# Value tiles of a first normalization: products taken by part, stage order and one load's queue changed

## Chip, core and metric

The kernel runs on one core of a Trainium2 chip, one launch of one program. The metric is the time of an execution on the device in microseconds (us), the median of several runs. Five engines work beside each other, each through its own instructions in order: TensorE (PE in the profile: matrix products and transposes, into PSUM banks), VectorE (DVE), ScalarE (ACT), GpSimd (POOL) and SyncE (SP, which here issues all DMAs).

## What is computed

The reference is one block of a streaming encoder in float32, over 1024 tokens and 16 meta tokens of 1024 channels:

```
u = rmsnorm(h, norm_mix)                    # h: 16 meta tokens, then 1024 tokens
z = u @ w_in                                # a, q, k, v, r, lr, ga, gb
y_a = pooling mixer of a;  y_b = chunked gated linear attention of q, k, v, lr, gated by r
h = h + (sigmoid(ga) * y_a + sigmoid(gb) * y_b) @ w_out
h = h + relu(rmsnorm(h, norm_ffn) @ w_ff1)^2 @ w_ff2
out = rmsnorm(h, norm_final)[16:]
```

The change lies in the first line and in the first columns of the second: the normalization of the tokens, and the products that make half of v (256 columns) and lr (16 columns).

## The kernel before

Each float32 operand is held as two parts, a high part (rounded by a ScalarE copy) and a low part (the rest, by a VectorE subtraction). A product takes three matmuls: high x high, high x low, low x high (`mm3`, L241 to L248). In the tables below `th`, `tl` are the high and low part of the normalized, transposed tokens, `vw` those of the value weights, `w1h`, `w1l` those of the gate weights.

The tokens come in eight tiles of 128 (t = 0 to 7; the 16 meta tokens are t = 8). One tile takes these steps:

- `squared(t)`: ScalarE squares the tile (1024 columns) and sums by row (L578); the next step of the same generator, `first_rms`, takes logarithm and exponential on ScalarE (L580, L581) and then a few operations on columns of one element (L582 to L590), on VectorE for t = 0 and 1, on GpSimd above that. The result is the row's scale `rs[t]`; `rest(t)` fetches it.
- `normed(t)`: VectorE multiplies the tile by `rs[t]` into one of three buffers `us` (L631), SP reloads its slot with tile t+4, TensorE transposes the tile in eight pieces into two banks (`turned`, L550).
- `taken(b, t)`: for each of the two banks VectorE multiplies by the norm's weights, a column per channel (`gcol`; L557, to `ut`), and ScalarE copies the high part (L566). It hands back the function that makes the low part on VectorE (L567).
- `v_tile(0, t)`: TensorE multiplies the tile by the value weights, 24 matmuls of 272 columns. It hands back two functions that copy the bank out on ScalarE (L497, L501).

ScalarE, VectorE and GpSimd run in the written order in this stage (`tc.manual_schedule`). In pass t of the loop the order is: the matmuls of tile t; `normed(t+2)`; the copying out of tile t-1; `rest(t+3)` (logarithm, exponential, small operations); `taken` of tile t+1; `squared(t+4)`; the low parts of tile t+1. Passes 5, 6 and 7 also split the first four pieces of gate weights (`q.prime`; L264 on ScalarE, L265 on VectorE). Before the loop stand tiles 0 and 1, the two dummy runs of transposes of the identity (`warm(12)`, `warm(10)`, L639), the transposing of the norm's weights into `gcol` (L656, L657), and the splitting of the value weights (`load_vw`: `hi` L455, `lo` L458, `lr` L462 and L463 for the low-rank columns).

SP issues, in this order at the start: tile 0, the identity, the norm's weights, tile 1, two blocks of value weights, the low-rank columns (`lrraw`, 1024 pieces of 64 bytes), tiles 2 and 3.

Behind the loop `differences` prepares the operands of a Strassen-like scheme for the gates: the tokens' quarters in `ut` are subtracted in place (`differ`, L726), and split into P5, P6, P7 and P4 (`halved`: L720 on ScalarE, L721 on VectorE). Between these steps `next(run)` issues one product each (`Quarters.run`): the split of the weights three products ahead, 12 matmuls, and evictions (L361).

Of the kernel before, what the change touches and what calls it, by code (L numbers as in the profile page):

```python
# [12 lines left out]
ALU = mybir.AluOpType  # L13
AX = mybir.AxisListType

P = 128
D = 1024
SEQ = 1024
META = 16
# [11 lines left out]
NPAIR = DFF // P // 2  # L31
MP = 264
PACE, LEVEL = 1.1, 1.6
WARM = (12, 10)


class Stack:
# [68 lines left out]
def kernel(  # L106
# [84 lines left out]
    def f32(ap):  # L191
        return ap.bitcast(F32)
# [256 lines left out]
    def load_vw(i, raws=None, parts=False):  # L449
        vw, raws = S["vw"][i], raws or fetch_vw(i)  # L450
        c = [slice(j * P, (j + 1) * P) for j in range(2)]
        eng = pool if i else dve

        def hi(j):
            act.activation(vw[:, 0, :, c[j]], raws[j], ACT.Copy)  # L455

        def lo(j):
            eng.tensor_tensor(vw[:, 1, :, c[j]], raws[j], f32(vw[:, 0, :, c[j]]), ALU.subtract)  # L458

        def lr():  # L460
            r = S["lrraw"]
            act.activation(vw[:, 0, :, 256:], r, ACT.Copy)  # L462
            dve.tensor_tensor(vw[:, 1, :, 256:], r, f32(vw[:, 0, :, 256:]), ALU.subtract)  # L463

        if parts:
            return hi, lo, lr
        for j in range(2):
            hi(j)
            lo(j)

    vm = gB[32 : 32 + META, : 2 * 256]

    def v_tile(i, t, later=False):

        vw, w = S["vw"][i], 256 + 16 * (i == 0)
        if t == 8:
            half, at, n = 0, 0, META
        else:
            half, n = t // 4, P
            at = OFF[half] + (t % 4) * P  # L480
        b = bank("mm")[:n, :w]
        th, tl, hi, lo = TH[half][:, :, at : at + n], TL[half][:, :, at : at + n], vw[:, 0], vw[:, 1]
        if i == t == 0:

            for k in range(KT):
                pe.matmul(b, th[:, k], hi[:, k], start=k == 0, stop=False)
                pe.matmul(b, tl[:, k], hi[:, k], start=False, stop=False)
            for k in range(KT):
                pe.matmul(b, th[:, k], lo[:, k], start=False, stop=k == KT - 1)
        else:  # L490
            mm3(b, KT, lambda k: (th[:, k], tl[:, k]), lambda k: (hi[:, k], lo[:, k]))

        def leave():
            if t == 8:
                act.activation(vm[:, i * 256 : i * 256 + 256], b[:, :256], ACT.Copy)
            else:
                act.activation(S["v"][i][:, t], b[:, :256], ACT.Copy)  # L497

        def leave_lr():
            if i == 0:  # L500
                act.activation(S["lrtok"][:n, t], b[:, 256:], ACT.Copy)  # L501

        if later:
            return leave, leave_lr
        leave()
        leave_lr()
# [64 lines left out]
    def first_rms(xt, u, eng):  # L571

        rows = xt.shape[0]
        rs_n[0] += 1
        k = rs_n[0] % 2
        ss = ln_stat[rs_n[0] % 4][:rows]
        y, v, t = (stat[2 * k][:rows, 4 * i : 4 * i + 1] for i in range(3))
        act.activation(u, xt, ACT.Square, accum_out=ss)  # L578
        yield ss
        act.activation(y, ss, ACT.Ln, scale=1.0 / D, bias=eps_t[:rows])  # L580
        act.activation(y, y, ACT.Exp, scale=-0.5)  # L581
        eng.tensor_scalar(v, ss, -0.5 / D, -0.5 * EPS, ALU.mult, ALU.add)  # L582
        if eng is dve:
            dve.scalar_tensor_tensor(t, v, y, y, ALU.mult, ALU.mult)
            dve.scalar_tensor_tensor(ss, t, 1.5, y, ALU.add, ALU.mult)
        else:
            eng.tensor_tensor(t, v, y, ALU.mult)
            eng.tensor_tensor(t, t, y, ALU.mult)
            eng.tensor_scalar(t, t, 1.5, None, ALU.add)
            eng.tensor_tensor(ss, t, y, ALU.mult)  # L590
        yield ss

    def start():
# [25 lines left out]
        nc.sync.dma_start(g8, norm_mix.rearrange("(k p) -> k p", p=P))  # L619
        load(1)  # L620
        raws = fetch_vw(0)
        nc.sync.dma_start(S["lrraw"], w_in[:, C_LR : C_LR + 16].rearrange("(k p) c -> p k c", p=P))
        load(2)
        load(3)
        m = lambda half, j: tuple(a[half][:, 4 * j : 4 * j + 4, OFF[half] : OFF[half] + HALF] for a in (TH, TL))
# [2 lines left out]
        def normed(t):  # L628

            x_, u = of(t)  # L630
            dve.tensor_scalar(u, x_, rs[t], None, ALU.mult)  # L631
            if t < 4:
                load(t + 4)
            return turned(u)

        def warm(n):

            for _ in range(n):
                pe.transpose(idle[:, :P], ident, ident)  # L639
# [4 lines left out]
        with tc.manual_schedule(engines={mybir.EngineType.Activation, mybir.EngineType.DVE, mybir.EngineType.Pool}):  # L644
            rs, rms, b, leave = {}, {}, {}, None

            def squared(t):
                rms[t] = first_rms(xm if t == 8 else xs[:, t % 4], us[: META if t == 8 else P, t % 3], pool if t > 1 else dve)
                next(rms[t])

            def rest(t):
                rs[t] = next(rms[t])

            warm(WARM[0])
            bg = bank("ms")
            pe.transpose(bg[:, :KT], g8, ident[:KT, :KT])  # L656
            dve.tensor_copy(gcol, bg[:, :KT])  # L657
            squared(0)
            rest(0)
            b[0] = normed(0)  # L660
            squared(1)
            part = taken(b[0], 0)
            lows = [next(part)]
            rest(1)
            lows.append(next(part))
            b[1] = normed(1)
            warm(WARM[1])
            for fn in lows:
                fn()
            hi, lo, lr = load_vw(0, raws, True)  # L670
            for j in range(2):
                hi(j)
                lo(j)
            lr()
            squared(2)
            rest(2)
            squared(3)
            for t in range(8):
                left_now, leave = leave or (nothing,) * 2, v_tile(0, t, True)
                if t < 6:  # L680
                    b[t + 2] = normed(t + 2)
                if t < 2:
                    q.load(t, 0)
                elif t == 2:
                    nc.sync.dma_start(xm, meta)
                    q.load(0, 1)
                    q.load(1, 1)
                    nc.sync.dma_start(mf, masks)
                elif t == 7:
                    dve.tensor_scalar(xm, xm, rs[8], None, ALU.mult)  # L690
                for fn in left_now:
                    fn()
                if t < 6:
                    rest(t + 3)
                lows = list(taken(b[t + 1], t + 1)) if t < 7 else []
                if t < 5:
                    squared(t + 4)
                for fn in lows:
                    fn()
                for n in {5: (0,), 6: (1, 2), 7: (3,)}.get(t, ()):  # L700
                    q.prime(n == 0)
            differ((0, 0), (1, 0), (0, 0))
            bm = bank("ms")[:, : 8 * META].rearrange("p (a b) -> p a b", a=8)
            for i in range(KT):
                pe.transpose(bm[:, i], xm[:, i * P : (i + 1) * P], ident[:META, :META])
            um = us[:, 0, : 8 * META].rearrange("p (a b) -> p a b", a=8)
            for j in range(2):
                weighted(um[:, 4 * j : 4 * j + 4], bm[:, 4 * j : 4 * j + 4], j)
            th, tl = (a[0][:, :, :META] for a in (TH, TL))
            act.activation(th, um, ACT.Copy)  # L710
            dve.tensor_tensor(tl, um, f32(th), ALU.subtract)
            pool.tensor_copy(mask, mf)
            differences(run, leave)
# [9 lines left out]
    def differ(to, a, b):  # L723
        for k in range(0, 4, 2):
            to_, a_, b_ = (S["ut"][j][:, k : k + 2] for j in (to, a, b))
            dve.tensor_tensor(to_, a_, b_, ALU.subtract)  # L726

    def differences(run, values):


        b11, b21, b12, b22 = (0, 0), (0, 1), (1, 0), (1, 1)
        left.pop_to(S["left_x"])
        halved("P5", b11)
        for fn in values:
            fn()
        next(run)
        leave = v_tile(0, 8, True)
        differ(b11, b22, b11)
        next(run)
        for fn in leave:  # L740
            fn()
        halved("P6", b11)
        next(run)
        differ(b12, b22, b12)
        lr_turn()
        next(run)
        right.pop_to(S["right_ut"][4])
        halved("P7", b12)
        next(run)
        differ(b21, b21, b11)  # L750
        right.pop_to(S["right_ut"][2])
        halved("P4", b21)
        next(run)
        right.pop_to(S["right_ut"][0])
# [380 lines left out]
    def part(i):  # L1135
        return slice(i * CH, (i + 1) * CH)
# [562 lines left out]
```

## Time and profile before

| | |
|---|---|
| median of 3 runs | 1243.65 us (1243.61 to 1248.66) |
| profiled execution | 1241.63 us |
| its span | 1239.6 us, 18265 instructions |
| busy in the span | PE 97%, DVE 69%, ACT 50%, POOL 5% |
| mean granted TensorE clock | 0.996 |

The profile's page has the shares of the span; the views of the trace answer for a stretch of it. A timeline row gives start and duration in us, engine, line, operation, what it writes and reads, how many are merged, and in brackets the engine's idle time before it with what ended it. A row of waits gives the total, the number and the longest. A row of stages (from:to) gives its length, each engine's busy time with the number of instructions, the granted TensorE clock, the DMA engines' busy share and GB/s.

### The profile page before, as it was taken

How to read it: one execution, taken by the hardware profiler on the slowest of the kernel's cores; microseconds unless marked ns; L12 is line 12 of the kernel's file. 1: busy time of each engine (PE TensorE's matmuls, PEld its weight loads, DVE VectorE, ACT ScalarE, POOL GpSimd, SP SyncE). 2: the span in 40 equal slices, each digit the busy share in tenths (PEclk: the TensorE clock that was granted, in tenths of full speed). 3: DMA queues.
4: the chain of work that ended last, by engine and by line, in shares of the span. 5: the costliest groups of instructions: out<-in, count | busy, mean ns of one | idle time of the engine just before them, and what ended most of it. 6: DMA issues, size and time to landing. Idle time of an engine off the chain costs nothing.

```text
span 1239.6 us, 18265 instructions
## 1 busy us (share of the span) xinstructions
PE 1206.1 (97%) x6816; PEld 1003.1 (81%) x6816; DVE 850.9 (69%) x1388; ACT 618.8 (50%) x1099; POOL 66.6 (5%) x74
## 2 busy tenths in 40 slices
PE   7999999999999999899999999999999999999997
PEld 6878888988887778688878888888887788888886
DVE  6896676654556676634896676776774877887686
ACT  6667567322446663412654454555553444444554
POOL 2100000001101015400000000000000000000000
PEclk9999999999999999899999999999999999999999
DMA  8033326146102247831244444444569863333432
GB/s 250 2 110 104 110 86 193 53 155 219 36 19 78 69 133 234 282 109 51 98 125 159 156 153 143 162 156 134 176 216 374 289 235 102 94 99 98 162 98 89
DMA packets 142680, 173.84 MB, mean 140 GB/s; under 512 B 10968, under 2 KB 82416, under 8 KB 142592
## 3 DMA queue, kind: packets, MB, share of 16 engines
q1 hardware_dynamic: 142592, 172.68, 43.3%
q8 instruction: 53, 0.87, 0.3%
q14 instruction: 35, 0.29, 0.1%
HBM read 119.17 MB, written 53.48 MB: 139 GB/s over the span
## 4 chain that ended last, share of the span: by engine, by line
PE 85%; DVE 8%; ACT 3%; DMA 2%; issue 2%; SPq 0%; DVEq 0%; ACTq 0%
PE b_mm L246 10%; PE b_mm L247 10%; PE b_mm L248 10%; PE b_ms L247 9%; PE b_ms L246 9%; PE b_ms L248 9%; PE b_x L248 8%; PE b_x L246 8%; PE b_x L247 8%; PE b_sc L1147 1%; PE b_ms L550 1%; PE b_mx L246 1%; PE b_m L1249 1%; PE b_mx L247 1%; PE b_mx L248 1%
## 5 line engine op out<-in xcount | busy, mean ns | idle before, releaser
L246 PE MATMUL b_mm<-th,w1h 128*128 128x512 f32 (+1 forms) x312 | 117.6, 377 | 1.9 <-DVE c L761 1.1
L247 PE MATMUL b_mm<-tl,w1h 128*128 128x512 f32 (+1 forms) x312 | 116.0, 372 | 0.6 <-DVE tl L1407 0.6
L248 PE MATMUL b_mm<-th,w1l 128*128 128x512 f32 (+1 forms) x312 | 115.8, 371 | 0.0
L246 PE MATMUL b_x<-th,w1h 128*128 128x512 f32 (+1 forms) x240 | 90.8, 378 | 0.0
L247 PE MATMUL b_x<-tl,w1h 128*128 128x512 f32 (+1 forms) x240 | 90.6, 378 | 0.0
L248 PE MATMUL b_x<-th,w1l 128*128 128x512 f32 (+1 forms) x240 | 90.3, 376 | 0.0
L264 ACT ACTIVATE w1h<-raw 128x512 fp32r<-128x512 f32 x96 | 59.6, 621 | 36.8 <-PE b_x L247 14.1
L265 DVE TENSOR_TENSOR w1l<-raw,w1h 128x512 fp32r<-128x512 f32 x96 | 65.6, 684 | 12.9 <-ACT w1h L264 12.9
L246 PEld LDWEIGHTS b_mm<-th,w1h 128*128 128x128 f32 x312 | 58.6, 188 | 13.7 <-issue 1.8
L264 ACT ACTIVATE w1h<-fs 128x512 fp32r<-128x512 f32 x72 | 45.4, 631 | 45.8 <-PE b_ms L247 31.5
L247 PEld LDWEIGHTS b_mm<-tl,w1h 128*128 128x128 f32 x312 | 58.6, 188 | 10.6 <-DVE tl L1407 0.9
L248 PEld LDWEIGHTS b_mm<-th,w1l 128*128 128x128 f32 x312 | 58.6, 188 | 10.3
L264 ACT ACTIVATE w1h<-bt 128x512 fp32r<-128x512 f32 x44 | 27.8, 632 | 67.7 <-issue 59.6
L265 DVE TENSOR_TENSOR w1l<-fs,w1h 128x512 fp32r<-128x512 f32 x72 | 49.3, 685 | 14.7 <-ACT w1h L264 14.6
L1556 DVE TENSOR_TENSOR bt<-w,w 128x512 f32<-128x512 f32 x80 | 54.6, 683 | 1.0 <-DMA w<-in_w_ff_dram 1.0
L248 PEld LDWEIGHTS b_x<-th,w1l 128*128 128x128 f32 x240 | 45.1, 188 | 8.4
L246 PEld LDWEIGHTS b_x<-th,w1h 128*128 128x128 f32 x240 | 45.0, 188 | 8.5
L247 PEld LDWEIGHTS b_x<-tl,w1h 128*128 128x128 f32 x240 | 45.1, 188 | 8.3
L264 ACT ACTIVATE fxh<-bt 128x512 fp32r<-128x512 f32 x36 | 22.8, 632 | 55.4 <-issue 48.1
L246 PE MATMUL b_ms<-wo,w1h 128*128 128x512 f32 x128 | 49.8, 389 | 0.0
L247 PE MATMUL b_ms<-wo,w1h 128*128 128x512 f32 x128 | 49.8, 389 | 0.0
L248 PE MATMUL b_ms<-wo,w1l 128*128 128x512 f32 x128 | 49.8, 389 | 0.0
(446 smaller groups left out, 3365.2 us busy)
## 6 DMA issues: line engine op xcount, KB each, us to landing
hf_dram<-h SPq DMA_DIRECT2D x112, 256.0 KB, 2.1
raw<-hf_dram SPq DMA_DIRECT2D x112, 256.0 KB, 2.7
w<-in_w_ff_dram SPq DMA_DIRECT2D x64, 256.0 KB, 4.9
raw<-in_w_in_dram SPq DMA_DIRECT2D x24, 512.0 KB, 4.9
raw<-in_w_ff_dram SPq DMA_DIRECT2D x16, 512.0 KB, 4.1
rawx<-in_w_ff_dram SPq DMA_DIRECT2D x16, 512.0 KB, 4.1
xs<-in_x_dram SPq DMA_DIRECT2D x8, 512.0 KB, 4.7
rawx<-in_w_in_dram SPq DMA_DIRECT2D x8, 512.0 KB, 4.7
```

The source lines that it names most:

```text
L246: pe.matmul(ps, ah, bh, start=first and i == 0, stop=False, skip_group_check=more)
L247: pe.matmul(ps, ah, bl, start=False, stop=False, skip_group_check=more)
L248: pe.matmul(ps, al, bh, start=False, stop=last and i == n - 1, skip_group_check=more)
L264: act.activation(hi, a, ACT.Copy)
L265: dve.tensor_tensor(lo, a, f32(hi), ALU.subtract)
L550: pe.transpose(b[j][:, i], u[:, (4 * j + i) * P : (4 * j + i + 1) * P], ident)
L1147: pe.matmul(b[to, e, j], kk[r, s], qq[r, s], start=True, stop=True, tile_position=(e * CH, u * CH))
L1249: pe.matmul(o[part(u), e, j], scc[part(u), e, j], v[part(u), j, e], start=j == 0, stop=False, tile_position=(u * CH, u * CH), skip_group_c ...
L1556: dve.tensor_tensor(bt, w, S["w2"][q[3:]][:, i], ALU.add if q[2] == "+" else ALU.subtract)
```

## The change

- `first_rms` yields once more, after logarithm and exponential, so that `squared`, `root` and `rest` are three steps. Tile 2's small operations go to VectorE too.
- Before the loop: dummy runs of 4, 8 and 12; the copy to `gcol` behind `normed(0)`; tile 1's root ahead of tile 0's high parts; the weights' high parts ahead, and their low parts behind the weighting of tile 1. The matmuls of tiles 0 and 1 are issued by part (high x high, low x high, high x low, eight each) among these steps, with `normed(2)` between them. Squares, roots and small operations of tiles 2 and 3 are there as well.
- The loop starts at t = 1. In pass t the order is now: the matmuls of tile t (t > 1); `normed(t+2)`; the copying out of tile t-1; `taken` of tile t+1; square, root and small operations of tile t+3; the low parts of tile t+1.
- `lrraw` is loaded by a DMA on GpSimd's queue.
- In `differences` the split of P6 comes one product earlier.

```diff
--- before.py
+++ after.py
@@ -31,7 +31,7 @@
 NPAIR = DFF // P // 2
 MP = 264
 PACE, LEVEL = 1.1, 1.6
-WARM = (12, 10)
+WARM = (4, 8, 12)
 
 
 class Stack:
@@ -460,7 +460,7 @@
         def lr():
             r = S["lrraw"]
             act.activation(vw[:, 0, :, 256:], r, ACT.Copy)
-            dve.tensor_tensor(vw[:, 1, :, 256:], r, f32(vw[:, 0, :, 256:]), ALU.subtract)
+            return lambda: dve.tensor_tensor(vw[:, 1, :, 256:], r, f32(vw[:, 0, :, 256:]), ALU.subtract)
 
         if parts:
             return hi, lo, lr
@@ -470,7 +470,7 @@
 
     vm = gB[32 : 32 + META, : 2 * 256]
 
-    def v_tile(i, t, later=False):
+    def v_tile(i, t, later=False, by_part=False):
 
         vw, w = S["vw"][i], 256 + 16 * (i == 0)
         if t == 8:
@@ -480,14 +480,16 @@
             at = OFF[half] + (t % 4) * P
         b = bank("mm")[:n, :w]
         th, tl, hi, lo = TH[half][:, :, at : at + n], TL[half][:, :, at : at + n], vw[:, 0], vw[:, 1]
-        if i == t == 0:
-
+        parts = {"hh": (th, hi), "lh": (tl, hi), "hl": (th, lo)}
+        left_of = {"n": 3}
+
+        def part(name):
+            left_of["n"] -= 1
+            l, r = parts[name]
             for k in range(KT):
-                pe.matmul(b, th[:, k], hi[:, k], start=k == 0, stop=False)
-                pe.matmul(b, tl[:, k], hi[:, k], start=False, stop=False)
-            for k in range(KT):
-                pe.matmul(b, th[:, k], lo[:, k], start=False, stop=k == KT - 1)
-        else:
+                pe.matmul(b, l[:, k], r[:, k], start=name == "hh" and k == 0, stop=left_of["n"] == 0 and k == KT - 1)
+
+        if not by_part:
             mm3(b, KT, lambda k: (th[:, k], tl[:, k]), lambda k: (hi[:, k], lo[:, k]))
 
         def leave():
@@ -500,6 +502,8 @@
             if i == 0:
                 act.activation(S["lrtok"][:n, t], b[:, 256:], ACT.Copy)
 
+        if by_part:
+            return part, (leave, leave_lr)
         if later:
             return leave, leave_lr
         leave()
@@ -579,6 +583,7 @@
         yield ss
         act.activation(y, ss, ACT.Ln, scale=1.0 / D, bias=eps_t[:rows])
         act.activation(y, y, ACT.Exp, scale=-0.5)
+        yield ss
         eng.tensor_scalar(v, ss, -0.5 / D, -0.5 * EPS, ALU.mult, ALU.add)
         if eng is dve:
             dve.scalar_tensor_tensor(t, v, y, y, ALU.mult, ALU.mult)
@@ -619,7 +624,7 @@
         nc.sync.dma_start(g8, norm_mix.rearrange("(k p) -> k p", p=P))
         load(1)
         raws = fetch_vw(0)
-        nc.sync.dma_start(S["lrraw"], w_in[:, C_LR : C_LR + 16].rearrange("(k p) c -> p k c", p=P))
+        pool.dma_start(S["lrraw"], w_in[:, C_LR : C_LR + 16].rearrange("(k p) c -> p k c", p=P))
         load(2)
         load(3)
         m = lambda half, j: tuple(a[half][:, 4 * j : 4 * j + 4, OFF[half] : OFF[half] + HALF] for a in (TH, TL))
@@ -645,7 +650,10 @@
             rs, rms, b, leave = {}, {}, {}, None
 
             def squared(t):
-                rms[t] = first_rms(xm if t == 8 else xs[:, t % 4], us[: META if t == 8 else P, t % 3], pool if t > 1 else dve)
+                rms[t] = first_rms(xm if t == 8 else xs[:, t % 4], us[: META if t == 8 else P, t % 3], pool if t > 2 else dve)
+                next(rms[t])
+
+            def root(t):
                 next(rms[t])
 
             def rest(t):
@@ -654,29 +662,51 @@
             warm(WARM[0])
             bg = bank("ms")
             pe.transpose(bg[:, :KT], g8, ident[:KT, :KT])
-            dve.tensor_copy(gcol, bg[:, :KT])
+            warm(WARM[1])
             squared(0)
+            root(0)
             rest(0)
             b[0] = normed(0)
+            dve.tensor_copy(gcol, bg[:, :KT])
             squared(1)
-            part = taken(b[0], 0)
-            lows = [next(part)]
+            root(1)
+            lows = [list(taken(b[0], 0))]
             rest(1)
-            lows.append(next(part))
+            warm(WARM[2])
             b[1] = normed(1)
-            warm(WARM[1])
-            for fn in lows:
+            hi, lo, lr = load_vw(0, raws, True)
+            hi(0)
+            hi(1)
+            lr_lo = lr()
+            v0, leave0 = v_tile(0, 0, by_part=True)
+            v1, leave = v_tile(0, 1, by_part=True)
+            v0("hh")
+            for fn in lows[0]:
                 fn()
-            hi, lo, lr = load_vw(0, raws, True)
+            v0("lh")
+            lows.append(list(taken(b[1], 1)))
+            v1("hh")
             for j in range(2):
-                hi(j)
                 lo(j)
-            lr()
+            lr_lo()
+            v0("hl")
             squared(2)
+            root(2)
             rest(2)
+            b[2] = normed(2)
+            v1("hl")
+            for fn in lows[1]:
+                fn()
+            v1("lh")
             squared(3)
-            for t in range(8):
-                left_now, leave = leave or (nothing,) * 2, v_tile(0, t, True)
+            root(3)
+            rest(3)
+            q.load(0, 0)
+            for t in range(1, 8):
+                if t > 1:
+                    left_now, leave = leave, v_tile(0, t, True)
+                else:
+                    left_now = leave0
                 if t < 6:
                     b[t + 2] = normed(t + 2)
                 if t < 2:
@@ -690,11 +720,11 @@
                     dve.tensor_scalar(xm, xm, rs[8], None, ALU.mult)
                 for fn in left_now:
                     fn()
+                lows = list(taken(b[t + 1], t + 1)) if t < 7 else []
                 if t < 6:
+                    squared(t + 3)
+                    root(t + 3)
                     rest(t + 3)
-                lows = list(taken(b[t + 1], t + 1)) if t < 7 else []
-                if t < 5:
-                    squared(t + 4)
                 for fn in lows:
                     fn()
                 for n in {5: (0,), 6: (1, 2), 7: (3,)}.get(t, ()):
@@ -736,10 +766,10 @@
         next(run)
         leave = v_tile(0, 8, True)
         differ(b11, b22, b11)
+        halved("P6", b11)
         next(run)
         for fn in leave:
             fn()
-        halved("P6", b11)
         next(run)
         differ(b12, b22, b12)
         lr_turn()
```

## The prediction

> **What bounds the kernel now.** I read the head of the profile's page, then TensorE's waits, then its busy time by stage.
>
> ```profile
> span 1239.6 us, 18265 instructions
> PE 1206.1 (97%) x6816; PEld 1003.1 (81%) x6816; DVE 850.9 (69%) x1388; ACT 618.8 (50%) x1099; POOL 66.6 (5%) x74
> ```
>
> TensorE is busy in all but 33.5 us of the span, and the change keeps every real product. It can only take from these 33.5 us, or add to them. Two views say where they lie near the change: waits (us in total, times, longest) and stages (from:to, length, busy time of each engine).
>
> ```profile
> PE b_ms L248 <- DVE w1l L265: 1.8, 1, 1.8
> ...
> PE b_mm L246 <- DVE c L761: 1.1, 1, 1.1
> ```
> ```profile
> 4.60:17.50 12.90, 8.49 (x38) 7.67 (x39) 7.31 (x16) 7.76 (x17) 0.33 (x1) 1.00 0.93 281
> 17.50:47.20 29.70, 29.70 (x244) 29.55 (x243) 26.58 (x42) 22.33 (x57) 10.75 (x37) 1.00 0.44 114
> 47.20:76.50 29.30, 27.58 (x139) 21.69 (x139) 25.65 (x33) 19.39 (x34) 0.00 (x0) 1.00 0.04 15
> ```
>
> The real products begin at about 17.5. From there to 47.2 (the eight value tiles) TensorE never stops; then it stops twice, 1.8 us at P4's product and 1.1 us behind a bank, both times for VectorE. So there are three places to look at: the start, the loop over tiles (full, so it can only lose), and the two stops.
>
> **1. The start: the normalization of tile 3 comes 2.8 us earlier.** Timeline rows: start, duration, engine, line.
>
> ```profile
> 6.00 0.20 ACT L581 ACTIVATE small<-small 128x1 f32<-128x1 f32 x1
> 7.70 0.17 DVE L657 COPY small<-b_ms 128x8 f32<-128x8 f32 x1 [6.83 <-PE b_ms L656]
> 7.79 0.14 DVE L582 TENSOR_SCALAR small<-small 128x1 f32<-128x1 f32 x1
> 8.05 0.22 DVE L584 SCALAR_TENSOR_TENSOR small<-small 128x1 f32<-128x1 f32 x1
> 8.50 0.75 DVE L631 TENSOR_SCALAR us<-xs,small 128x1024 f32<-128x1024 f32 x1
> 9.31 1.97 PE L550 MATMUL b_ms<-ident,us 128*128 128x128 f32 x8 [1.64 <-DVE us L631]
> 13.85 1.99 ACT L455 ACTIVATE vw<-raw 128x1024 fp32r<-128x1024 f32 x2
> 15.06 2.35 DVE L458 TENSOR_TENSOR vw<-raw,vw 128x1024 fp32r<-128x1024 f32 x2
> 15.95 1.04 ACT L578 ACTIVATE us<-xs 128x1024 f32<-128x1024 f32 x1
> 17.55 1.04 ACT L578 ACTIVATE us<-xs 128x1024 f32<-128x1024 f32 x1
> 18.85 0.75 DVE L631 TENSOR_SCALAR us<-xs,small 128x1024 f32<-128x1024 f32 x1 [1.23 <-POOL small L590]
> ```
>
> The root of tile 0 is ready at 6.2, but VectorE first waits for the copy of the weights' column (7.70), behind 12 dummy transposes. The change moves that copy behind the normalization. From L584 to L631 is 0.45, so normalization 0 starts at about 6.7, 1.8 earlier; its transposes, 0.81 later, at 7.5, end at 9.5. The second half is weighted by 10.2, three small operations (7.79 to 8.50: 0.71) give normalization 1 at 10.9, and its transposes stand by 12.7. Meanwhile ScalarE makes the weights' high parts, 1.99, from 10.8 to 12.8, and the low-rank columns. VectorE takes the low parts of tile 0 (1.28) to 12.8 and then weights tile 1. By the loop's rows below (26.03 to 27.88) the next square starts 1.85 later, at 14.65; the square after it 1.60 later (15.95 to 17.55), at 16.25; and from a square to its normalization by way of GpSimd it is 2.90 (15.95 to 18.85). By ScalarE, then, normalization 3 could start at 19.15. VectorE has ahead of it: tile 1 weighted (to 14.05), the weights' low parts and the low-rank ones (2.35 and 0.25, to 16.65), tile 2's small operations, which leave GpSimd (0.71, to 17.4), normalization 2 (0.66, to 18.05), tile 1's low parts (1.28). That is **19.3**, which I take; before it was 22.11.
>
> The 24 dummies (22 before) lie where TensorE is idle (8.49 of 12.90 us busy, and 22 dummies are in that): nothing. Were the 12 behind tile 0 still at 0.21 each (1.97 for eight, against 1.04 below), tile 1's transposes would be some 0.4 late, under VectorE's 1.28: nothing either.
>
> Tiles 0 and 1 by part: the same 48 products in another order, at a time when normalization 3, not TensorE, sets what comes next: nothing. One gate weight's load is issued before the loop, not in it; its split is at 38.71 (below): nothing.
>
> The low-rank load: its row in the DMA view (KB, us to landing), and its issue.
>
> ```profile
> lrraw<-in_w_in_dram SPq DMA_DIRECT2D x1, 64.0 KB, 7.2
> ```
> ```profile
> 3.54 3.02 SPq L622 DMA_DIRECT2D lrraw<-in_w_in_dram  x1
> ```
>
> SP is spared 3.02 us of issue, and tiles 2 and 3 load that much earlier; but the square of tile 2 (15.95) shows no wait for its load, so that is worth nothing. On GpSimd's queue I take the same 7.2 us from about 1.1, behind its first memsets: 8.3, against a need at 12.8. Bounds: nothing, or, beyond 4.5 us of delay, one for one, because ScalarE works in order and the first product, tile 1 and the next squares stand behind that copy.
>
> [...]
>
> **2. The loop: it loses its look-ahead.** Before, pass t squares tile t+4 and takes the root of tile t+3, squared one pass ago. After, pass t does square, roots and GpSimd's operations of tile t+3, all behind ScalarE's copies of tile t+1; and the first thing VectorE does in pass t+1 is normalization t+3. That is an added wait. Behind it on VectorE stand the weighting and the low parts of tile t+2, for which TensorE's tile t+2 waits.
>
> ```profile
> 20.70 1.04 PE L550 MATMUL b_ms<-ident,us 128*128 128x128 f32 x8
> 22.11 0.75 DVE L631 TENSOR_SCALAR us<-xs,small 128x1024 f32<-128x1024 f32 x1
> 24.56 1.04 PE L550 MATMUL b_ms<-ident,us 128*128 128x128 f32 x8
> 25.37 0.75 DVE L631 TENSOR_SCALAR us<-xs,small 128x1024 f32<-128x1024 f32 x1
> 26.03 1.28 DVE L557 TENSOR_TENSOR ut<-b_ms,small 128x512 f32<-128x512 f32 x2
> 27.88 1.04 ACT L578 ACTIVATE us<-xs 128x1024 f32<-128x1024 f32 x1
> 35.55 0.75 DVE L631 TENSOR_SCALAR us<-xs,small 128x1024 f32<-128x1024 f32 x1
> 38.71 0.62 ACT L264 ACTIVATE w1h<-rawx 128x512 fp32r<-128x512 f32 x1
> 39.78 0.68 DVE L265 TENSOR_TENSOR w1l<-rawx,w1h 128x512 fp32r<-128x512 f32 x1
> 40.11 1.03 PE L550 MATMUL b_ms<-ident,us 128*128 128x128 f32 x8
> 40.75 1.29 DVE L557 TENSOR_TENSOR ut<-b_ms,small 128x512 f32<-128x512 f32 x2 [0.29 <-PE b_ms L550]
> ```
>
> A pass now takes TensorE (40.11 - 24.56) / 4 = 3.89. The new circle: normalization to the square behind the copies, 25.37 to 27.88 = 2.51; square to the normalization that it feeds, 2.90; together **5.41**. No step of it overlaps another, since every engine works in order. So normalization 7 starts at 19.3 + 4 x 5.41 = 40.95 (before 35.55), the square of pass 5 at 43.45. Then in order: the split of the first gate weight on ScalarE, 1.60 later at 45.05, 0.62; its low part on VectorE, 0.6 to the next; the weighting of tile 7 at about 46.35 instead of 40.75. VectorE is **5.6** us late. TensorE's tile 7 waits for its low parts (46.35 + 1.28 + 0.1 + 0.64 = 48.35), and 21 products remain. A pass of 3.89, less 1.0 of transposes, by 24 gives 0.12 for one: the last starts at 50.9, against 40.11 + 1.0 + 48 x 0.12 = 46.9 before, **4.0** late.
>
> **3. P6's split: VectorE gets 2.5 us back.**
>
> ```profile
> 52.63 2.35 DVE L726 TENSOR_TENSOR ut<-ut,ut 128x1024 f32<-128x1024 f32 x2
> 55.51 0.68 DVE L265 TENSOR_TENSOR w1l<-fs,w1h 128x512 fp32r<-128x512 f32 x1
> 58.76 2.36 DVE L721 TENSOR_TENSOR P6l<-ut,P6h 128x1024 fp32r<-128x1024 f32 x2 [2.57 <-ACT P6h L720]
> 63.07 0.40 PE L246 MATMUL b_mm<-P5h,w1h 128*128 128x512 f32 x1
> 76.57 0.51 PE L248 MATMUL b_ms<-P4h,w1l 128*128 128x512 f32 x1 [1.78 <-DVE w1l L265]
> 80.26 0.47 PE L246 MATMUL b_mm<-th,w1h 128*128 128x512 f32 x1 [1.10 <-DVE c L761]
> ```
>
> P6h stood on ScalarE behind two evictions that waited for TensorE; now it follows the difference (52.63), half by half, and VectorE's wait of 2.57 shrinks to about 0.1. The split of P5's weights falls behind it by 2 us; its product is at 63.07, its split ended at 56.2 (55.51 + 0.68): covered. VectorE feeds both stops of TensorE, so what counts at 76.57 is VectorE's lateness: 5.6 - 2.5 = 3.1. TensorE by itself would be 4.0 - 1.8 = 2.2 late there. The later decides: **+3.1**. The stop behind the bank moves along, and what follows keeps its relative order.
>
> **The sum.** Start -2.8 and loop +8.4 on VectorE make +5.6; P6 -2.5; so +3.1 us. The profiled execution, 1241.63 (span 1239.6 and 2.03 around it), would be 1244.7. The median of the runs shown is 1243.65, 2.0 above it; on it I forecast **1246.8**, slower by 0.25%. I call 0.5% (6.2 us) about what a measurement of this kernel can tell from no change, so this counts as the same.
>
> **Rivals.**
> - *TensorE stays the bound of the loop.* That needs ScalarE's squares to run ahead of the copies in front of them; all of the trace's rows are in program order, which speaks against it. Then tile 2's normalization at 17.4, transposes at 18.2 to 19.25, 16 products of 0.12, and tile 3's transposes at 21.2 instead of 24.56: -3.3, and both stops gone (-2.9): 1237.4. 12%.
> - *P6's move gives nothing*, because P6h now waits for TensorE in another way or VectorE's idle time returns before P4: +5.6, 1249.3. 12%.
> - *The clock falls in the loop* (ends slower). A circle of 5.41 leaves TensorE 1.4 us idle per pass. The trace shows one drop:
>
> ```profile
> 515.00:527.00 12.00, 6.76 (x19) 4.49 (x19) 9.23 (x9) 5.33 (x7) 3.80 (x3) 0.72 0.92 305
> ```
> ```profile
> 521.25 0.79 PE L246 MATMUL b_mm<-wo,th 128*128 128x512 f32 x1 [2.83 <-ACT wo L1345]
> ```
>
> There TensorE was 56% busy, its gaps up to 2.83, and the granted clock averaged 0.72: 12 x 0.28 = 3.4 us lost. In the loop it would be 3.9 / 5.41 = 72% busy with gaps of about 1 us. If that sufficed it would cost 3.4 on top: 1250.2. It decides as soon as the busy share falls near 56%. 10%.
>
> [...]
> - *The low-rank load lands late* (ends slower): beyond 12.8 one for one; 4 us more give 1250.8. 8%.
>
> **How the numbers follow.** My forecast has 58%, by itself 1244 to 1249 (the profiled execution and the median differ by 2.0, and the circle by 0.2 a pass). With the second rival, part of the third and some of the fourth the range 1242 to 1251 holds 8 in 10; below it lies the first rival, above it the rest of the last two. Faster than 1237.4: half the first rival, 6%. Slower than 1249.9: most of the third and of the fourth, and the ends of the second and of the forecast, 17%. The rest, 77%, is the same.
>
> **What the changed profile would show.** Right: normalizations (L631) near 6.7, 10.9 and 19.3, then one every 5.4 us, each ended by GpSimd; TensorE waiting about 1.5 us a pass from tile 3 on; no wait at P6l; P4's wait under 1 us, near 79.7. Wrong: tile transposes every 3.9 us; ScalarE waiting for lrraw; products of 0.25 us in the loop; a wait of more than 2 us still at P4.

## The result, and the profile after

The changed kernel takes 1248.44 us (median of 22 runs, 1245.84 to 1251.81); the kernel before, run beside it, 1245.62 (22 runs). The ratio is **1.0021, 95% interval 1.0012 to 1.0031**: 2.6 us slower (1.5 to 3.9). The forecast was +3.1 us. In what follows line numbers are those of the changed kernel, 4 or 5 higher at the start and 30 higher behind the loop.

The head of the page of the changed kernel; its execution took 1250.37 us.

```profile
span 1248.6 us, 18265 instructions
PE 1211.1 (97%) x6818; PEld 1004.1 (80%) x6818; DVE 852.0 (68%) x1391; ACT 618.5 (50%) x1099; POOL 63.9 (5%) x70
```

This span is 9.0 us longer than the one before, over three times what the medians differ by. So the two spans aren't compared; I follow one instruction of both traces instead, the product behind the bank at P4, which was at 80.26. TensorE's timeline after:

```profile
67.98 0.40 PE L246 MATMUL b_mm<-P5h,w1h 128*128 128x512 f32 x1
...
80.18 0.50 PE L248 MATMUL b_ms<-P4h,w1l 128*128 128x512 f32 x1 [0.70 <-DVE w1l L265]
...
83.88 0.47 PE L246 MATMUL b_mm<-th,w1h 128*128 128x512 f32 x1 [1.13 <-DVE c L791]
```

P5's first product is 4.91 us later than before (63.07), P4's third 3.61 (76.57), the one behind the bank 3.62. From there the shift hardly moves: +3.54 at about 500 us. That is what the change costs, and the medians agree with it. The stages, as in the prediction:

```profile
4.60:17.50 12.90, 11.05 (x73) 9.78 (x73) 9.83 (x23) 10.63 (x23) 0.36 (x1) 1.00 1.06 337
17.50:47.20 29.70, 25.80 (x185) 22.70 (x184) 18.55 (x30) 16.60 (x44) 6.79 (x31) 1.00 0.38 94
47.20:76.50 29.30, 28.13 (x151) 22.61 (x152) 28.03 (x37) 19.44 (x36) 0.47 (x2) 1.00 0.00 1
```

At the start TensorE does more (73 matmuls for 38), in the loop's stage less: 185 for 244, with all of 29.70 us busy before. VectorE's timeline shows why:

```profile
6.99 0.75 DVE L636 TENSOR_SCALAR us<-xs,small 128x1024 f32<-128x1024 f32 x1
...
10.58 0.75 DVE L636 TENSOR_SCALAR us<-xs,small 128x1024 f32<-128x1024 f32 x1
...
19.44 0.75 DVE L636 TENSOR_SCALAR us<-xs,small 128x1024 f32<-128x1024 f32 x1 [0.67 <-POOL small L595]
...
24.86 0.75 DVE L636 TENSOR_SCALAR us<-xs,small 128x1024 f32<-128x1024 f32 x1 [2.07 <-POOL small L595]
...
41.32 0.75 DVE L636 TENSOR_SCALAR us<-xs,small 128x1024 f32<-128x1024 f32 x1 [2.14 <-POOL small L595]
...
46.76 1.28 DVE L561 TENSOR_TENSOR ut<-b_ms,small 128x512 f32<-128x512 f32 x2
...
58.63 2.35 DVE L756 TENSOR_TENSOR ut<-ut,ut 128x1024 f32<-128x1024 f32 x2
61.04 2.36 DVE L751 TENSOR_TENSOR P6l<-ut,P6h 128x1024 fp32r<-128x1024 f32 x2
...
64.64 0.69 DVE L317 TENSOR_TENSOR fs<-fs,rawx 128x512 f32<-128x512 f32 x1
```

Each normalization of the loop now begins after an idle stretch of about 2.1 us that GpSimd ends, 5.42 to 5.50 us after the last one. The chain that ends last, asked for the stretch to 50 us, walks once round the circle per pass:

```profile
24.86 0.75 DVE us L636
25.61 0.61 DVE ut L561
26.25 1.23 ACT th L570 x2
27.47 1.05 ACT us L582 x2
30.34 0.75 DVE us L636
```

Normalize, weight, copy the high parts, square the next tile, its scale (the stretch from 28.5 to 30.34, too small pieces for this list), normalize again: no TensorE in it. TensorE's own idle time shows far less of it:

```profile
PE b_ms L554 <- DVE us L636: 3.4, 6, 1.0
PE b_mm L248 <- DVE tl L571: 1.3, 6, 0.2
```

In the loop that is 0.52 to 0.58 and 0.21 us a pass (the 1.0 belongs to tile 1, ahead of the loop), though a pass takes 1.6 us more than before. The other half hides in the modelled ends: a product lasts 0.29 us in the records and the next starts 0.125 later, so of the 0.50 us between the starts at 27.16 and 27.66 only 0.21 counts as idle. The starts of two equal instructions tell the pass's length; the idle column doesn't.

### The profile page after: what moved, and what is told of

Read it like the earlier page. It is cut to its first block, busy times and chain, and to the rows that moved or that the text cites. A ratio compares the mean times of both kernels' runs of the same rounds, so it can differ in the third digit from the quotient of the medians.

```text
span 1248.6 us, 18265 instructions
## 1 busy us (share of the span) xinstructions
PE 1211.1 (97%) x6818; PEld 1004.1 (80%) x6818; DVE 852.0 (68%) x1391; ACT 618.5 (50%) x1099; POOL 63.9 (5%) x70
## 4 chain that ended last, share of the span: by engine, by line
PE 83%; DVE 9%; ACT 4%; DMA 2%; issue 1%; POOL 0%; SPq 0%; ACTq 0%; DVEq 0%; POOLq 0%
PE b_mm L246 10%; PE b_mm L247 9%; PE b_mm L248 9%; PE b_ms L246 9%; PE b_ms L247 9%; PE b_ms L248 9%; PE b_x L248 8%; PE b_x L246 8%; PE b_x L247 8%; PE b_sc L1177 1%; PE b_mx L246 1%; PE b_mx L247 1%; PE b_mx L248 1%; DMA raw<-hf_dram 1%; DVE ut L756 1%
```

## Experiments

The theory: **the loop's lost look-ahead makes the circle of 5.4 us, and P6's earlier split gives part of it back at P4.** The rivals: the cost is at the start (the load on GpSimd's queue, the dummies); or P6's move does nothing; or the price lies in the clock. Each run is read twice: by its ratio to the kernel before, and by the shift of the product behind the bank (before 80.26).

**a_ahead: the change with the look-ahead given back.**

```diff
             rest(3)
+            squared(4)
             q.load(0, 0)
...
-                lows = list(taken(b[t + 1], t + 1)) if t < 7 else []
                 if t < 6:
-                    squared(t + 3)
                     root(t + 3)
                     rest(t + 3)
+                lows = list(taken(b[t + 1], t + 1)) if t < 7 else []
+                if t < 5:
+                    squared(t + 4)
```

> The changed kernel with the look-ahead given back: tile 4 squared before the loop, then in pass t the roots and small operations of tile t+3 ahead of the copies of tile t+1, and the square of tile t+4 behind them. Theory (the circle of the loop costs what is lost): normalizations 3.9 us apart instead of 5.4, TensorE without waits in the loop, P4's third product some 6 us ahead of the kernel before (near 70.5 instead of 76.57), time 5 to 6 us below before, ratio about 0.9955. Rival (the products by part or the load on GpSimd's queue cost it): that product stays behind the kernel before, near 79 to 80, ratio about 1.002.

Measured: 1238.71 us (5 runs) against 1243.68 (15), ratio **0.9957 (0.9944 to 0.997)**. Its profile, in turn VectorE's normalizations, TensorE's timeline, and one stretch of the loop:

```profile
22.94 0.75 DVE L636 TENSOR_SCALAR us<-xs,small 128x1024 f32<-128x1024 f32 x1
26.20 0.75 DVE L636 TENSOR_SCALAR us<-xs,small 128x1024 f32<-128x1024 f32 x1
```
```profile
59.96 0.40 PE L246 MATMUL b_mm<-P5h,w1h 128*128 128x512 f32 x1
...
71.30 0.39 PE L248 MATMUL b_ms<-P4h,w1l 128*128 128x512 f32 x1
...
74.77 0.47 PE L246 MATMUL b_mm<-th,w1h 128*128 128x512 f32 x1 [1.04 <-DVE c L793]
```
```profile
20.00:43.00 23.00, 22.79 (x186) 22.50 (x185) 21.82 (x35) 17.54 (x44) 7.92 (x27) 1.00 0.39 96
```

The waits for GpSimd are gone, normalizations follow every 3.26 us (3.9 was expected; VectorE runs ahead of TensorE), and TensorE is busy in 22.79 of 23.00 us. P5's first product is 3.11 us earlier than before (the start's gain, kept through the loop), and P4's stop has vanished too: -5.49 behind the bank. A few moved lines turn 3.6 us lost into 5.5 gained. The loop's order is the cost, and the rest of the change is worth having.

**c_loop: the loop's new order alone, in the kernel before.**

```diff
             squared(3)
+            rest(3)
...
-                if t < 6:
-                    rest(t + 3)
                 lows = list(taken(b[t + 1], t + 1)) if t < 7 else []
-                if t < 5:
-                    squared(t + 4)
+                if 0 < t < 6:
+                    squared(t + 3)
+                    rest(t + 3)
```

> The kernel before with only the order of the loop changed: square, roots and small operations of tile t+3 all behind the copies of tile t+1 in pass t, none ahead; tile 3's are done before the loop. Theory: normalizations 5.4 us apart from tile 3 on, normalization 7 near 43.7 instead of 35.55, P4's third product 8.3 us late (near 84.9), ratio about 1.0067. Rival (the loop hides most of the circle): under 3 us late, ratio under 1.0025.

Measured: 1250.63 us (4 runs) against 1243.68, ratio **1.0054 (1.0041 to 1.0068)**. Normalizations, then P4's third product:

```profile
22.18 0.75 DVE L631 TENSOR_SCALAR us<-xs,small 128x1024 f32<-128x1024 f32 x1
27.66 0.76 DVE L631 TENSOR_SCALAR us<-xs,small 128x1024 f32<-128x1024 f32 x1 [2.15 <-POOL small L590]
```
```profile
84.27 0.51 PE L248 MATMUL b_ms<-P4h,w1l 128*128 128x512 f32 x1 [1.80 <-DVE w1l L265]
```

The same circle, 5.48 us, from the old start: P4 is 7.70 late, the product behind the bank 7.71 (87.97), and +8.1 remain at about 500 us; somewhat less than the 8.3 expected, since VectorE's wait at P6l is 1.48 here instead of 2.57. (A clock drop at 85 us, with products 0.43 us apart for 0.23 and a granted clock of 0.93 over 76.5 to 100, stands here in place of the bank's stop.) With the old start and the old place of P6's split little else pays it back.

**d_no_p6: the change with P6's split at its old place.**

```diff
-        halved("P6", b11)
         next(run)
         for fn in leave:
             fn()
+        halved("P6", b11)
```

> The changed kernel with the split of P6 put back to its old place. Theory: VectorE has no wait of 2.57 us to lose, P4's third product comes 2.5 us later than in the changed kernel (near 82.7), ratio to the kernel before 1.0045. Rival (the move gives nothing): as the changed kernel, 80.2, ratio 1.002.

Measured: 1250.43 us (4 runs) against 1243.68, ratio **1.0054 (1.0039 to 1.007)**. VectorE at P6, TensorE at P4:

```profile
63.92 2.36 DVE L751 TENSOR_TENSOR P6l<-ut,P6h 128x1024 fp32r<-128x1024 f32 x2 [1.48 <-ACT P6h L750]
```
```profile
81.73 0.51 PE L248 MATMUL b_ms<-P4h,w1l 128*128 128x512 f32 x1 [1.80 <-DVE w1l L265]
```

P4 comes at 81.73, 5.16 after the kernel before; the prediction's sum without P6 was 5.6. The changed kernel has it at 80.18, 1.55 earlier; at about 500 us the difference is 1.82 (shift +5.36 against +3.54, with a clock drop at 82 to 85 us in this run, products 0.43 us apart for 0.23). But 0.25 of it is there at normalization 3 (19.69 for 19.44), far ahead of the edit, and stays up to P5's first product (68.23 for 67.98): the move is worth 1.3 at P4. The ratios, 1.0054 and 1.0021, are 4 us apart, but their intervals allow from 1 to 7. VectorE's wait for P6h is 1.48 here, not the 2.57 of the kernel before: VectorE arrives 6 us later, TensorE only 5, and with it the evictions that held P6h up. The wait had already shrunk.

**b_p6: P6's split moved, in the kernel before.** The same edit as in d_no_p6, the other way round.

> The kernel before with only the split of P6 moved forward. Theory: VectorE's wait of 2.57 us at P6l goes, P4's third product comes 1.8 us earlier without a wait and the stop behind the bank shrinks as well, together 2.5 to 2.9 us, ratio about 0.998. Rival (the move gives nothing): VectorE waits elsewhere before P4, ratio 1.000.

Measured: 1241.86 us (11 runs) against 1243.68, ratio **0.9982 (0.9973 to 0.9991)**.

```profile
74.61 0.39 PE L248 MATMUL b_ms<-P4h,w1l 128*128 128x512 f32 x1
...
78.06 0.47 PE L246 MATMUL b_mm<-th,w1h 128*128 128x512 f32 x1 [1.03 <-DVE c L761]
```

P4's stop of 1.78 has gone, and the whole is 2.20 earlier, somewhat less than the 2.5 to 2.9 expected: as the stop is gone, TensorE itself sets the limit. The rival that P6's move gives nothing falls.

**e_lr_sp and f_ahead_lr_sp: the low-rank load back on SP's queue**, in the change and in a_ahead.

```diff
-        pool.dma_start(S["lrraw"], w_in[:, C_LR : C_LR + 16].rearrange("(k p) c -> p k c", p=P))
+        nc.sync.dma_start(S["lrraw"], w_in[:, C_LR : C_LR + 16].rearrange("(k p) c -> p k c", p=P))
```

> The changed kernel with the low-rank load back on SP's queue. In the changed kernel tile 1's square waits 1.46 us for its load. Theory (that wait is off the path, since VectorE and GpSimd set normalization 3): the square of tile 1 starts near 6.4 instead of 7.96, normalization 3 stays near 19.2 to 19.4, P4's third product moves by less than 0.4 us, ratio to the kernel before 1.002 to 1.0025. Rival (the load on GpSimd's queue is part of the loss): everything behind it comes 1 to 1.5 us earlier, ratio about 1.001.

> The changed kernel with the look-ahead given back and the low-rank load back on SP's queue. Theory: TensorE is the bound there, its first product waits 0.7 us for the low-rank columns behind tile 1's late square, so some 0.5 us less than with the look-ahead alone, ratio to the kernel before 0.9950 to 0.9957. Rival (the queue doesn't matter): the same as with the look-ahead alone, 0.9957.

Measured: e 1248.42 us (10 runs) against 1245.11 (19), ratio **1.0028 (1.0015 to 1.0041)**; f 1240.02 (4 runs), ratio **0.9955 (0.9937 to 0.9972)**. The product behind the bank is at 84.26 in e (changed kernel 83.88) and at 74.95 in f (a_ahead 74.77). The 0.38 of e is there at normalization 1 (10.96 for 10.58) and doesn't grow; d_no_p6, with the load on GpSimd's queue, has normalizations 1 and 3 within 0.14 of e's (10.83 and 19.69 for 10.96 and 19.83). So there is no gain, and no loss that these runs can tell: the queue of this load is off the path, also where the loop has its look-ahead. The gain of 0.5 expected for f isn't there. Tile 1's square came at 7.37 in e, not at 6.4: it still waits 1.13 for its own load. In the changed kernel's DMA view and GpSimd's timeline it reads:

```profile
lrraw<-in_w_in_dram POOLq DMA_DIRECT2D x1, 64.0 KB, 5.2
```
```profile
1.27 1.10 POOL L627 DMA_DIRECT2D lrraw<-in_w_in_dram  x1 [0.44 <-issue]
```

It is there by about 6.5 us; ScalarE wants it at 12.51.

**g_small_dve: another way round the circle.** All small operations on VectorE, behind the low parts, in the loop's new order.

```diff
-                rms[t] = first_rms(xm if t == 8 else xs[:, t % 4], us[: META if t == 8 else P, t % 3], pool if t > 2 else dve)
+                rms[t] = first_rms(xm if t == 8 else xs[:, t % 4], us[: META if t == 8 else P, t % 3], dve)
...
                     squared(t + 3)
                     root(t + 3)
-                    rest(t + 3)
                 for fn in lows:
                     fn()
+                if t < 6:
+                    rest(t + 3)
```

> The changed kernel with every tile's small operations on VectorE, in pass t behind the low parts of tile t+1: a shorter circle, look-ahead still lost. Theory: 2.51 from normalization to square, 1.72 to the end of the exponential, 0.5 for two small operations, together 4.7 us a pass instead of 5.47; four passes give 3 us, P4's third product near 77.2 instead of 80.18, ratio to the kernel before 0.9995 to 1.0005. Rival (the loop is held by ScalarE's load or by TensorE, not by the circle): passes stay at 5.4 and the ratio at 1.002.

Measured: 1245.4 us (10 runs) against 1245.11, ratio **0.9998 (0.9987 to 1.0009)**.

```profile
19.59 0.75 DVE L636 TENSOR_SCALAR us<-xs,small 128x1024 f32<-128x1024 f32 x1
...
24.30 0.75 DVE L636 TENSOR_SCALAR us<-xs,small 128x1024 f32<-128x1024 f32 x1
...
38.70 0.75 DVE L636 TENSOR_SCALAR us<-xs,small 128x1024 f32<-128x1024 f32 x1
```
```profile
77.50 0.50 PE L248 MATMUL b_ms<-P4h,w1l 128*128 128x512 f32 x1 [0.69 <-DVE w1l L265]
```

The circle is 4.7 to 5.0 us instead of 5.4 to 5.5. Normalization 7 comes at 38.70 instead of 41.32, 2.62 earlier, and P4 2.68 earlier than in the changed kernel: the loss follows the length of the circle, as the theory has it.

**h_no_dummies: the change without the 12 dummies behind tile 0** (one execution, so no ratio).

```diff
-WARM = (4, 8, 12)
+WARM = (4, 8, 0)
```

> The changed kernel without the third run of 12 dummy transposes. Theory: they lie in TensorE's idle time and cost nothing; without them tile 1's transposes may run at half clock, and normalization 3 stays near 19.4, P4's third product within 0.3 us of 80.2. Rival (they keep the clock up and their loss is felt): products of tiles 0 and 1 take 0.23 us each instead of 0.125, normalization 3 and P4 come 1 us or more later.

Measured: 1249.67 us; P4 at 81.02, 0.84 later than in the changed kernel. TensorE by stages, first the changed kernel, then this one:

```profile
10.00:12.00 2.00, 0.99 (x10) 0.75 (x9) 1.81 (x6) 2.00 (x4) 0.00 (x0) 1.00 1.06 397
12.00:14.00 2.00, 1.62 (x14) 1.38 (x13) 2.00 (x4) 1.64 (x4) 0.00 (x0) 1.00 1.05 406
```
```profile
10.00:12.00 2.00, 0.27 (x2) 0.27 (x3) 1.82 (x6) 1.98 (x4) 0.00 (x0) 1.00 1.02 386
12.00:14.00 2.00, 1.42 (x10) 1.19 (x9) 2.00 (x5) 1.84 (x4) 0.00 (x0) 0.69 0.98 391
14.00:16.00 2.00, 2.00 (x11) 2.00 (x10) 2.00 (x3) 1.97 (x5) 0.00 (x0) 0.50 1.01 363
```

Without them the granted clock falls at about 12.8 us (0.69 over 12 to 14, 0.50 over 14 to 18), and the first eight products take 2.18 us instead of 1.27. But not all of the 0.84 is theirs. Tile 0's transposes, which stand ahead of these dummies, were slower in this run (the changed kernel's row, then this one's):

```profile
7.95 1.12 PE L554 MATMUL b_ms<-ident,us 128*128 128x128 f32 x8
```
```profile
7.74 1.84 PE L554 MATMUL b_ms<-ident,us 128*128 128x128 f32 x8
```

With that, normalizations 1 and 3 are both 0.35 late (10.93 and 19.79). The other 0.48 comes behind normalization 3, in the first pass of the loop (5.90 for 5.42), where VectorE waits 0.40 for transposes that stand behind the slow products. So the dummies save about 0.5 us here: more than the 0.3 expected, less than the rival's 1.

## Why the prediction was right, step by step

- **Start, right (-2.67 for -2.8), by two errors that cancel, one of them luck.** Normalizations 0, 1 and 3 came at 6.99, 10.58 and 19.44 (forecast 6.7, 10.9, 19.3). The squares of tiles 2 and 3 were 0.3 us earlier than worked out, which is the luck: tile 0's transposes took 1.12 us in this execution, where the forecast had them end at 9.5, as slow as before (1.97). In a_ahead, d, e, f and h they took 1.84 to 1.92, and normalization 3 came at 19.68 to 19.86, a gain of 2.25 to 2.43. On the other side, from tile 3's square (15.91) to its normalization it took 3.53 us, not 2.90: VectorE idled 0.67 for GpSimd, whose operations were slow just there:

```profile
17.14 0.48 POOL L587 TENSOR_SCALAR small<-small 128x1 f32<-128x1 f32 x1 [14.43 <-ACT us L582]
17.74 0.48 POOL L592 TENSOR_TENSOR small<-small 128x1 f32<-128x1 f32 x1
18.30 0.52 POOL L593 TENSOR_TENSOR small<-small 128x1 f32<-128x1 f32 x1
...
29.28 0.19 POOL L592 TENSOR_TENSOR small<-small 128x1 f32<-128x1 f32 x1 [0.49 <-ACT small L585]
```
```profile
16.82 0.75 DVE L636 TENSOR_SCALAR us<-xs,small 128x1024 f32<-128x1024 f32 x1
17.49 1.29 DVE L571 TENSOR_TENSOR tl<-ut,th 128x512 fp32r<-128x512 f32 x2
```

  Three operations of 0.48 to 0.52 us beside VectorE's, against 0.19 while VectorE is idle (29.28). The first ends at 17.62, VectorE's normalization at 17.57; the second at 18.22, VectorE's first low part at 18.18; the third at 18.82, VectorE's second low part at 18.78: 0.3 us lost each time. In the trace of before, from 17 to 35 us, GpSimd's operations that start inside a normalization or a low part take 0.31 to 0.75 us (0.75 at 18.90, inside the normalization of 18.85), those inside a weighting 0.19 to 0.21 (0.19 at 19.73, inside the one of 19.52). What holds them up no run shows. The first loss hides behind ScalarE's exponential (to 17.61); the other two make the 0.63.
- **Loop, right.** The circle is 5.42 to 5.50 (5.41), normalization 7 at 41.32 (40.95), VectorE's weighting of tile 7 at 46.76 (46.35): 6.0 late for 5.6, within the 0.2 a pass left for the circle. The sign "TensorE waiting about 1.5 us a pass" shows in the passes' length (5.42 to 5.50 for 3.89), not in the recorded waits (about 0.8).
- **TensorE's own lateness, too small.** I had 4.0 behind tile 7, its last product at 50.9; it came at 51.63, after a start at 48.89 for 48.35, and P5's first product shows 4.91. By TensorE alone P4 would be 4.91 - 1.78 = 3.1 late, not 2.2. VectorE, 3.6 late there (its low part at 79.44 for 75.83), still decides: TensorE waits 0.70.
- **P6, right in the sum, too large as the price of the move.** VectorE's lateness falls from 6.00 (the difference, 58.63 for 52.63) to 3.60 (the first step after P6l and both splits of weights, L317, 64.64 for 61.04). So 2.4 came back for 2.5, and the sum is 6.0 - 2.4 = 3.6 for 5.6 - 2.5 = 3.1: 0.4 of the missing 0.5 is the loop's. But d_no_p6 shows that 1.1 of the 2.4 comes back without the move, because the lateness itself shortens the wait at P6l from 2.57 to 1.48. The move alone is worth 1.3, and without it P4 would be 4.9 late (5.16 less 0.25 at the start), not the 5.6 of the second rival. I took the wait at its size in the old trace, where an edit ahead of it had changed when both sides arrive.
- **Rivals.** TensorE as the loop's bound needs the look-ahead: with it (a_ahead) the price worked out, -6.2, came near (-5.5). The load was early, not late. The clock didn't fall in the loop: 1.00, with TensorE 25.80 of 29.70 us busy and recorded idle stretches of at most 0.6. In h_no_dummies it fell to 0.50 behind a gap of 2.16 us and 1.1 us of transposes; what decides it no run shows.

Left open: the 0.5 us of the dummies rest on one execution, and why tile 0's transposes are fast in one execution and slow in another no run shows.

## What to carry to other kernels

When a step is moved behind the work that consumes its predecessor, add up the circle it closes (from its result, through each in-order engine, back to its next start) and compare it with the pass of the bounding engine: 5.4 against 3.9 us made a look-ahead of one tile worth 9 us here, more than all the rest of the change. Size the stall that an edit removes as it will be after the other edits, not as the old trace shows it. And where single executions wander, follow one instruction through both traces instead of comparing spans, and one ahead of the edit as well: 0.25 to 0.35 us of what d_no_p6 and h_no_dummies seemed to show was there before the edit could act. The version that beats both kernels is a_ahead (0.9957; with the load on SP, 0.9955, not to be told apart).

## What the runs showed of the hardware

The granted clock drops late in the program, in part at places that vary from run to run and not with the change. All ten profiled runs have a drop between 515 and 535 us, six have one more between 938 and 954. In the changed kernel's profiled run:

```profile
520.00:534.00 14.00, 8.27 (x21) 5.96 (x22) 9.41 (x10) 5.85 (x7) 2.53 (x2) 0.63 0.91 291
...
944.00:956.00 12.00, 9.83 (x35) 7.39 (x34) 4.67 (x7) 3.75 (x7) 0.00 (x0) 0.86 1.00 376
```

In the profiled run of the kernel before, the second place kept its clock:

```profile
940.00:950.00 10.00, 8.86 (x38) 6.97 (x38) 3.97 (x6) 3.65 (x6) 0.00 (x0) 1.00 1.03 390
```

By (1 - clock) x length the changed kernel's run lost 5.2 and 1.7 us there, that of before 3.4 and nothing: 3.5 of the 5.5 us by which the spans differ beyond the shift at 500 us. The rest is about what two waits of TensorE grew by: the longest one for `wo`, 4.06 us instead of 2.83 (4.0 to 4.1 in seven other runs too, 2.89 in a_ahead), and the one for `fxh` at 948, 2.17 us instead of 1.14.

At the second place that wait tells the runs apart. In the six with the drop (the changed kernel, a_ahead, b_p6, e, f, h) TensorE waited 1.77 to 3.83 us for `fxh`, in the four without it (the kernel before, c_loop, d, g) 0.84 to 1.34; in all ten, ScalarE's step that makes it had itself waited for a load (2.73 us in the kernel before, 3.77 in the changed one). The length of one wait doesn't tell them apart everywhere, though. c_loop and d_no_p6 have a drop at 82 to 88 us, behind P4's stop of 1.80, and the kernel before has none behind 1.78; g_small_dve has one at 633 to 637 behind waits of 0.95 and 0.63, where the kernel before waits 0.85 and 0.64 and keeps its clock. What decides there stays open. Summed in the same way, over stretches of 2 us, the drops cost 3.4 us in the kernel before (518 to 528), 5.1 and 1.7 in the changed kernel (522 to 534, 950 to 954) and 3.4 in h_no_dummies (12 to 20): in these three runs steps of about 1.7. In stretches of 0.2 us, the drop of 1.7 is a clock of 0.50 from 950.2 to 953.6, 3.4 us.
